# Down projection's operand blocks issued by ScalarE from the second product on, and the out projection's second-half additions with priority

## The chip, the cores and the metric

The kernel runs on one core of one Trainium2 chip. The metric is device microseconds of one execution. Matrix products run on TensorE (PE in the profile), the other arithmetic on VectorE (DVE), ScalarE (ACT) and GpSimd (POOL). Transfers between memory and on-chip buffers are issued here by SyncE (SP, its queue is q1 in the profile) and by ScalarE (queue q10). Each engine runs its own instructions in order, and an instruction waits at its place until what it depends on is done. The time before the change is the median of three runs, 1108.88 us (1105.74 to 1109.55).

## The reference

One layer over 1024 tokens of width 1024: a combined projection feeds two kinds of attention, whose outputs are normed and concatenated (`mix`). After that comes what this study is about:

```python
h = h + jnp.einsum('bse,ed->bsd', mix, w_out[l])
hn = rmsnorm(h, norm_ffn[l])
h = h + conv_gated_mlp(hn, w_gate[l], w_up[l], conv_w[l], conv_b[l], w_down[l])
...
return rmsnorm(h, norm_final)
```

with (the depthwise convolution shortened to one name)

```python
g = jnp.einsum('bsd,df->bsf', h, w_gate)
u = jnp.einsum('bsd,df->bsf', h, w_up)
g = conv_of_width_3(g) + conv_b
return jnp.einsum('bsf,fd->bsd', jax.nn.silu(g) * u, w_down)
```

where `D_FF` is 2816. Everything is float32.

## The kernel before

**Layout and arithmetic.** Activations are held transposed: a tile is 128 features by 1024 tokens, and `tsl(h)` is one half of the tokens (512). A float32 product is made of three fast ones: both operands are split into a high part (ScalarE, a copy that rounds) and a low part (VectorE, the difference), and TensorE does high times high, high times low and low times high (lines 826 to 828 in `group`, 134 to 136 in `block`). So each operand block costs one ScalarE and one VectorE instruction before TensorE may use it.

**Stages.** Attention fills the first 400 us or so. The out projection's second half follows: for each half of the tokens and each of eight output tiles `d`, twelve matmuls go into one PSUM bank (banks with the tags "o", "s" and "pj" in turn, two of each), and `settle_out` adds the bank to the residual `h1` on VectorE (line 845), writes it to memory (ScalarE's queue, line 846) and squares it for the norm (848, 850). Between these, VectorE and ScalarE already scale the first half of the tokens by the norm (855) and split it into operands (833, 834) for the gated MLP, whose first products `p1` write banks "x" with the tag "pj".

The gate and up projections run next over 22 tiles of the wide layer, as seven products instead of eight by sums of halves (a Strassen-Winograd step, with VectorE's additions). Each finished tile is written to memory as operand blocks `X` for the down projection (`keep`, line 1020, on ScalarE's queue).

**The down projection** runs from about 878 us to the end, as seven products again (`PRODUCTS`). Each product is 4 output tiles `j` times 11 operand blocks, in groups `(p, j, c)` of 4, 4 and 3 blocks (`PARTS`), three matmuls per block. The first product goes through all `j` for each part, so that it can begin while its operand blocks are still made; the later ones finish one `j` after another. The second product goes on adding to the banks of the first, after ScalarE has copied the first product out of them (`leave`, line 1254). Later bank contents are added to the residual on VectorE (line 1221).

For each group the loop calls, in program order: `prepare(i + 6, i + 4)`, which issues weight loads (`raw`, line 1107, three buffers) up to six groups ahead and splits weights (815 on ScalarE, 816 on VectorE, nine buffers) up to four groups ahead; the matmuls; the eviction of the group before; a reload of the residual (1207) or its addition (1210); and for the next product `x_load(p + 1, q)` and `x_split(p + 1, q - 1)`. `x_load` brings one block of 128 x 512 into the second half of a buffer `xd` (line 1131), and `x_split` makes the high part (1137, ScalarE) and the low part (1138, VectorE). The `xd` blocks use 22 buffers in turn, so a block for product `p + 1` goes into the buffer of a block of product `p - 1` and waits for TensorE's last use of that.

**What sets the order.** TensorE's order is that of the program, by hand (`manual_schedule`). On every other engine a scheduler decides the order when the program is built; `high_priority` moves an instruction ahead of others that are ready. Transfers from both queues share eight completion counters in turn, so an issue waits for the transfer that used its counter before it.

Of the kernel before, what the change touches and what calls it, by code (L numbers as in the profile page):

```python
# [16 lines left out]
ALU = mybir.AluOpType  # L17
PSUM = bass.MemoryType.PSUM

D, S, HD = 1024, 1024, 64  # L20
KT = D // 128
NB = S // 128
HALF = 512
# [30 lines left out]
def hybrid_layer(tc, xT, w_in, w_out, w_gate, w_up, w_down, small, sink, rpb, consts, rope, out):  # L54
    nc = tc.nc
    with ExitStack() as ctx:
# [13 lines left out]
        def big(name, tag, dt=F32):  # L70
            return lpool.tile([128, S], dt, name=name, tag=tag, bufs=slots[tag])
# [4 lines left out]
        def bank(name, tag):  # L76
            return psum.tile([128, HALF], F32, name=name, tag=tag)

        f32 = lambda ap: ap.bitcast(F32)
# [499 lines left out]
        t = quarters(big("f", "mix"))  # L579
# [106 lines left out]
        for g in range(2):  # L686
            for b in range(NB):
                q, t = unit_window(g, b)
# [49 lines left out]
        for u in range(len(flat)):  # L738
            q, t, need, kind = flat[u]
# [101 lines left out]
        at = lambda k, h: h1[k][:, tsl(h)]  # L841

        def settle_out():
            d, h, ps = late.pop(0)
            nc.vector.tensor_tensor(at(d, h), ps, at(d, h), op=ALU.add)
            nc.scalar.dma_start(spilled[d][:, tsl(h)], at(d, h))
            s2 = half("s2")
            nc.scalar.activation(s2, at(d, h), AF.Square)
            if total[h] is not None:
                nc.vector.tensor_tensor(s2, s2, total[h], op=ALU.add)  # L850
            total[h] = s2
# [34 lines left out]
        for h in range(2):  # L886
            for d in range(KT):
                if h == 0 and d + 2 < KT:
                    wo.append(load_wo(d + 2, fpool))
                ps = bank("pj", ("o", "s", "pj")[(h * KT + d) % 3])  # L890
                for _ in product(ps, wo[d], mg[4:8], h):
                    pass
                late.append((d, h, ps))
                if h == 1 and d == 1:
                    v = inverse_narrow([total[0]], D, "pt")
                settle_out()
                if h == 0 and d in (3, 4):
                    pure((0, FT // 2)[d - 3])
                if h == 0 and d >= 5 or h == 1 and d == 0:
                    head_weights((d - 5) % KT, "s1")  # L900
                if h == 1 and d == 2:
                    wide = widen(v, "pt")
                    normed(0, wide, K1)
                    B[1, 1] = [operand(at(k, 0), "xg") for k in K1]
                if h == 1 and d == 4:
                    normed(0, wide, K2)
                    B[2, 1] = [operand(at(k, 0), "xg") for k in K2]
# [108 lines left out]
        X, first_of = {}, {}  # L1016
# [73 lines left out]
        PRODUCTS = [("11", "11"), ("12", "21"), ("s1", "t1"), ("s2", "t2"), ("s4", "22"), ("s3", "t3"), ("22", "t4")]  # L1090
# [37 lines left out]
        def x_load(p, k):  # L1128
            t = big("xd", "xg" if counts[0] % (2 * FH) < 16 else "op", F32R)
            counts[0] += 1  # L1130
            nc.sync.dma_start(f32(t[:, HALF:S]), X[PRODUCTS[p][1], k])
            xraw[p, k] = t

        def x_split(p, k):
# [18 lines left out]
        for i, f in enumerate(FO[HEAD:]):  # L1153
# [19 lines left out]
            if last_one:  # L1173
                for k in range(4):
                    x_load(0, k)
# [3 lines left out]
            if last_one:  # L1179
                for k in range(4, 6):  # L1180
                    x_load(0, k)
                u.p7()
# [5 lines left out]
            if not last_one:  # L1188
                u.p7()
            else:  # L1190
                for k in range(4):
                    x_split(0, k)
                prepare(4, 2)
                for k in range(6, FH):
                    x_load(0, k)
# [76 lines left out]
        for i, (p, j, c) in enumerate(order):  # L1272
# [6 lines left out]
            ps = banks[p, j]  # L1279
# [26 lines left out]
        for k, cols in enumerate(quarters):  # L1306
            for j in (2, 3):
                ps = banks[6, j]
# [109 lines left out]
```

## Time and profile before

| | |
|---|---|
| time of the profiled execution | 1108.75 us |
| its span | 1106.7 us |
| TensorE's mean granted clock | 0.995 |
| median of three runs | 1108.88 us |
| TensorE idle, 900 to 950 us | 2.76 us |
| TensorE idle, 450 to 460 us | 1.06 us |
| TensorE idle, 1050 us to the end | 7.4 us |
| ScalarE busy, 900 to 950 us | 23.88 us |
| VectorE busy, 470 to 520 us | 49.53 us of 50 |
| ScalarE's waits for `xd` transfers (L1137) | 59.1 us in 35 waits |
| DMA engines' busy share, 900 to 950 us | 0.90, 289 GB/s |
| DMA engines' busy share, 700 to 750 us | 0.30, 101 GB/s |

The profile is of one execution. Busy time leaves out instructions that only wait or issue transfers. A line of the timeline gives the start, the duration, the engine, the source line, the operation and in brackets how long the engine had been idle before it and what released it. A line of the windows gives a stretch of time and its length, then for PE, PEld, DVE, ACT and POOL the busy time and number of instructions, then TensorE's granted clock, the DMA engines' share and GB/s. A line of the waits gives engine, what waited, what it waited for, the sum, how often and the longest. "To landing" is the time from issue of a transfer to its completion.

### The profile page before, as it was taken

To read this page: it belongs to the slowest core of one execution; us is meant where nothing else is said; L and a number is where in the kernel's file an instruction comes from. 1 tells how busy PE (TensorE), PEld (TensorE's weight loads), DVE (VectorE), ACT (ScalarE), POOL (GpSimd) and SP (SyncE) were. 2 spreads that over 40 slices of the span, in tenths; PEclk is the share of its full clock that TensorE was granted. 3 is DMA by queue.
4 is the path that set the end of the run, shared out by engine and by line. 5 is a ranking of instruction groups with operands and counts; after the bars stand their busy time and mean duration, and the time that the engine had idled before them with its cause. 6 is when DMAs were issued, how large, how long until landed. Compare 5 with 4: busy or idle time off the path is not lost.

```text
span 1106.7 us, 15054 instructions
## 1 busy us (share of the span) xinstructions
PE 1082.4 (98%) x5190; PEld 903.6 (82%) x5190; DVE 857.7 (77%) x1565; ACT 551.6 (50%) x1041; POOL 108.7 (10%) x188
## 2 busy tenths in 40 slices
PE   9989999999999999999999999999999999999997
PEld 7868888888888888787788888888888878888887
DVE  7478888667688687899988877877887868886844
ACT  7257766656666544454444334342434644544531
POOL 2213333222232100000000000000000000000001
PEclk9999999999999999999999999999999999999999
DMA  7213122232225237304433222323322889874734
GB/s 270 71 51 79 49 66 65 70 86 67 77 64 156 68 106 264 106 11 145 167 121 127 105 105 96 113 97 116 104 86 105 272 287 300 267 224 159 270 95 153
DMA packets 68364, 144.94 MB, mean 131 GB/s; under 512 B 8128, under 2 KB 18880, under 8 KB 68288
## 3 DMA queue, kind: packets, MB, share of 16 engines
q1 hardware_dynamic: 57632, 118.16, 34.4%
q10 hardware_dynamic: 10656, 25.82, 6.2%
q8 instruction: 40, 0.66, 0.2%
q14 instruction: 36, 0.29, 0.1%
HBM read 103.58 MB, written 28.57 MB: 119 GB/s over the span
## 4 chain that ended last, share of the span: by engine, by line
PE 84%; DVE 9%; DMA 3%; ACT 2%; issue 2%; ACTq 0%; POOL 0%; SPq 0%; DVEq 0%; POOLq 0%
PE dn L826 6%; PE pj L134 6%; PE dn L828 6%; PE dn L827 6%; PE pj L135 6%; PE pj L136 6%; PE z L828 5%; PE z L826 5%; PE z L827 5%; PE s L309 3%; PE x L826 3%; PE x L827 3%; PE x L828 3%; PE y L828 3%; PE y L827 3%; PE y L826 3%
## 5 line engine op out<-in xcount | busy, mean ns | idle before, releaser
L826 PE MATMUL dn<-xd,whi 128*128 128x512 f32 (+1 forms) x330 | 124.9, 378 | 2.8 <-ACT c L1254 2.8
L828 PE MATMUL dn<-xd,wlo 128*128 128x512 f32 (+1 forms) x330 | 124.2, 376 | 0.0
L827 PE MATMUL dn<-xd,whi 128*128 128x512 f32 (+1 forms) x330 | 124.2, 376 | 0.0
L815 ACT ACTIVATE whi<-ws 128x512 fp32r<-128x512 f32 (+1 forms) x100 | 60.1, 623 | 124.1 <-DVE ws L932 82.5
L134 PE MATMUL pj<-xgh,whi 128*128 128x512 f32 x248 | 104.6, 422 | 3.1 <-DVE t L189 3.1
L828 PE MATMUL z<-hg,wlo 128*128 128x512 f32 x264 | 103.1, 390 | 0.6 <-DVE wlo L816 0.6
L826 PE MATMUL z<-hg,whi 128*128 128x512 f32 x264 | 103.0, 390 | 0.2 <-DVE gs L982 0.2
L827 PE MATMUL z<-hg,whi 128*128 128x512 f32 x264 | 102.7, 389 | 0.0
L335 ACT ACTIVATE p<-p,nm 128x385 f32<-128x385 f32 (+3 forms) x128 | 74.9, 586 | 46.9 <-DVE nm L331 46.2
L136 PE MATMUL pj<-xgh,wlo 128*128 128x512 f32 x248 | 98.3, 396 | 0.0
L135 PE MATMUL pj<-xgl,whi 128*128 128x512 f32 x248 | 98.0, 395 | 0.0
L339 POOL TENSOR_SCALAR p<-p,sm 128x384 f32<-128x384 f32 (+1 forms) x128 | 73.4, 586 | 222.0 <-DVE sm L337 207.4
L816 DVE TENSOR_TENSOR wlo<-raw,whi 128x512 fp32r<-128x512 f32 (+1 forms) x102 | 66.3, 670 | 21.8 <-ACT whi L815 20.9
L345 DVE TENSOR_TENSOR pl<-pt,ph 128x384 fp32r<-128x384 f32 (+2 forms) x108 | 63.0, 588 | 24.8 <-ACT ph L344 23.7
L815 ACT ACTIVATE whi<-raw 128x512 fp32r<-128x512 f32 (+1 forms) x102 | 60.4, 611 | 41.7 <-DMA raw<-in_w_down_dram 19.0
L816 DVE TENSOR_TENSOR wlo<-ws,whi 128x512 fp32r<-128x512 f32 (+1 forms) x100 | 66.7, 681 | 18.4 <-ACT whi L815 18.3
L1137 ACT ACTIVATE xd<-xd 128x512 fp32r<-128x512 f32 x77 | 47.1, 627 | 59.4 <-DMA xd<-x 59.1
L1245 POOL TENSOR_TENSOR h<-h,wide 128x256 f32<-128x256 f32 (+1 forms) x6 | 5.4, 925 | 719.8 <-ACT wide L1241 719.8
L826 PEld LDWEIGHTS dn<-xd,whi 128*128 128x128 f32 x330 | 62.5, 189 | 14.2 <-ACT c L1254 3.2
L827 PEld LDWEIGHTS dn<-xd,whi 128*128 128x128 f32 x330 | 62.6, 190 | 11.2
L828 PEld LDWEIGHTS dn<-xd,wlo 128*128 128x128 f32 x330 | 62.4, 189 | 11.4
L344 ACT ACTIVATE ph<-pt 128x384 fp32r<-128x384 f32 (+2 forms) x108 | 55.0, 513 | 32.7 <-PE pt L444 25.2
(209 smaller groups left out, 2687.8 us busy)
## 6 DMA issues: line engine op xcount, KB each, us to landing
xd<-x SPq DMA_DIRECT2D x77, 256.0 KB, 5.0
raw<-in_w_down_dram SPq DMA_DIRECT2D x72, 256.0 KB, 4.1
raw<-in_w_gate_dram SPq DMA_DIRECT2D x22, 512.0 KB, 3.5
raw<-in_w_up_dram SPq DMA_DIRECT2D x22, 512.0 KB, 3.6
x<-c ACTq DMA_DIRECT2D x22, 512.0 KB, 2.6
raw<-in_w_in_dram SPq DMA_DIRECT2D x32, 256.0 KB, 2.8
raw<-in_w_down_dram SPq DMA_DIRECT2D x36, 192.0 KB, 3.9
x<-t ACTq DMA_DIRECT2D x11, 512.0 KB, 2.6
```

What stands on the lines that cost most here:

```text
L134: nc.tensor.matmul(ps, w[0], x[0][:, tsl(h)], start=first, stop=False)
L135: nc.tensor.matmul(ps, w[0], x[1][:, tsl(h)], start=False, stop=False)
L136: nc.tensor.matmul(ps, w[1], x[0][:, tsl(h)], start=False, stop=last)
L335: nc.scalar.activation(p[:, j, 0:e], p[:, j, 0:e], AF.Exp, bias=nm, scale=-1.0, accum_out=sm[:, j:j + 1])
L339: nc.gpsimd.tensor_scalar(p[:, i, 0:m], p[:, i, 0:m], sm[:, i:i + 1], 1.0, op0=ALU.mult, op1=ALU.mult)
L344: nc.scalar.activation(ph[:, 0:n], ps[:, 0:n], AF.Copy)
L345: nc.vector.tensor_tensor(pl[:, 0:n], ps[:, 0:n], f32(ph[:, 0:n]), op=ALU.subtract)
L815: nc.scalar.activation(hi, src, AF.Copy)
L816: nc.vector.tensor_tensor(lo, src, f32(hi[:, :, :]), op=ALU.subtract)
L826: nc.tensor.matmul(ps, w[0], x[0], start=first and i == 0, stop=False, skip_group_check=True)
L827: nc.tensor.matmul(ps, w[0], x[1], start=False, stop=False, skip_group_check=True)
L828: nc.tensor.matmul(ps, w[1], x[0], start=False, stop=last and i == len(ws) - 1, skip_group_check=True)
```

## The change

Two places. In the out projection's second half, the addition of a finished bank to the residual gets a high priority, as the additions of the first half have. In the down projection, the loads of the operand blocks are issued by SP for the first product and by ScalarE for the six others (66 of 77 loads).

```diff
         def settle_out():
             d, h, ps = late.pop(0)
-            nc.vector.tensor_tensor(at(d, h), ps, at(d, h), op=ALU.add)
+            with tc.high_priority(offset=500):
+                nc.vector.tensor_tensor(at(d, h), ps, at(d, h), op=ALU.add)
             nc.scalar.dma_start(spilled[d][:, tsl(h)], at(d, h))
...
         def x_load(p, k):
             t = big("xd", "xg" if counts[0] % (2 * FH) < 16 else "op", F32R)
             counts[0] += 1
-            nc.sync.dma_start(f32(t[:, HALF:S]), X[PRODUCTS[p][1], k])
+            (nc.scalar if p else nc.sync).dma_start(f32(t[:, HALF:S]), X[PRODUCTS[p][1], k])
             xraw[p, k] = t
```

TensorE's and GpSimd's orders are the same in both programs. VectorE's and ScalarE's orders differ in the second half of the out projection and in the down projection, SP's in the down projection.

## The prediction

> **What bounds the kernel now.** I read the page's busy table first, then TensorE's waits, the timeline and the windows round its two largest waits outside the attention, and last the transfers.
>
> ```profile
> PE 1082.4 (98%) x5190; PEld 903.6 (82%) x5190; DVE 857.7 (77%) x1565; ACT 551.6 (50%) x1041; POOL 108.7 (10%) x188
> PE dn L826 <- ACT c L1254: 2.8, 1, 2.8
> PE x L826 <- DVE h L845: 1.1, 1, 1.1
> ```
>
> TensorE is the bound: 98% of 1106.7 us, so idle time is only 24.3 us in all. The two waits are the only ones above 1 us from 400 us on, and each edit touches one: L1254 evicts the down projection's first product, L845 is the addition in the out projection's second half.
>
> ```profile
> 906.82 0.63 ACT L1137 ACTIVATE xd<-xd 128x512 fp32r<-128x512 f32 x1 [2.42 <-DMA xd<-x]
> 909.76 0.63 ACT L1137 ACTIVATE xd<-xd 128x512 fp32r<-128x512 f32 x1 [1.79 <-DMA xd<-x]
> 910.30 0.58 ACT L1254 ACTIVATE c<-dn 128x512 f32<-128x512 f32 x1
> 910.93 0.79 PE L826 MATMUL dn<-xd,whi 128*128 128x512 f32 x1 [2.76 <-ACT c L1254]
> 911.52 0.63 PE L827 MATMUL dn<-xd,whi 128*128 128x512 f32 x1
> 904.00:908.00 4.00, 4.00 (x19) 3.12 (x17) 1.72 (x3) 1.55 (x3) 0.00 (x0) 1.00 0.88 273
> 908.00:912.00 4.00, 1.24 (x4) 0.88 (x4) 2.35 (x5) 2.24 (x5) 0.00 (x0) 0.82 0.86 263
> 912.00:916.00 4.00, 4.00 (x15) 3.22 (x14) 3.49 (x7) 2.92 (x6) 0.00 (x0) 0.75 0.92 284
> ```
>
> The eviction had nothing to wait for but its place: it stands behind operand splits, and these wait for transfers. TensorE starts at 910.93 and not at 908.01 (the last matmul began at 907.78, pitch 0.227). The granted clock then falls to 0.75; the pitch is 0.43 until 913.65. The eighth matmul of the second product starts at 914.05 and would have at 909.60: **4.45 us lost**.
>
> ```profile
> 452.55 2.49 DVE L834 TENSOR_TENSOR hg<-h,hg 128x512 fp32r<-128x512 f32 x4
> 454.96 1.88 DVE L845 TENSOR_TENSOR h<-pj,h 128x512 f32<-128x512 f32 x3
> 456.30 0.50 PE L826 MATMUL x<-hg,whi 128*128 128x512 f32 x1 [1.05 <-DVE h L845]
> ```
>
> Three additions stand behind four operand splits. The second of them frees the bank of the next x product, which starts at 456.30 and not at 455.08: **1.22 us lost**.
>
> **Part one, priority.** No work is added; only VectorE's and ScalarE's order changes. In the built order each of the last six additions stands between the scalings (L855, 0.66 us) and splits (L834, 0.60 us). From the wait at 440.06 I add 0.60 to 0.66 per instruction: the addition of d=6 ends near 452.6, 2.5 us ahead of the need at 455.08. What is pushed back: the last split of the second operand set ends at 457.0 instead of 455.0, and TensorE reaches it at 457.8 plus three blocks of 0.68, 459.8; so that costs nothing, and 2.8 us late it would begin to. The sum of squares for the second norm ends near 460.6; TensorE is there at 460.5 (462.23 before): 0.1 lost. The sums for the next weights now wait for two loads issued behind it, which puts the second norm's reciprocal at 463.6 against a need at 464.2. Bounds: gain 0 (VectorE, 9.9 of 10 us busy from 470 on, returns the wait later) to 1.3. I take **-1.2**, since VectorE's own idle time before 467 (2.65 us at 437, four pieces from 458 to 466) is what shrinks.
>
> **Part two, the queue.** 66 of the 77 operand loads (256 KB) go from SP to ScalarE.
>
> Issue cost: a load of this kind takes 0.32 to 0.43 us on SP; 66 of them are 21 to 28 us of ScalarE over 190 us, where it is half idle (24.3 busy of 50 us at 1000 to 1050). A store issued at 870.76 between splits that start at 870.75 and 871.29 shows no gap at all. 0 to 0.4 each, I take 0.1, hidden by that idle time; without cover 0.4 times 11, 4.4 us per product.
>
> The order costs more. In the built order ScalarE issues block N+1, splits block N (waiting for its landing), splits one set of weights, issues N+2. So two blocks take one landing time L plus one operand split and one weight split (0.55 each in a row of splits):
>
> two blocks = L + 1.1; eleven blocks = 5.5 x (L + 1.1).
>
> A product is 132 matmuls at 0.227, 29.9 us. ScalarE keeps up while L is under **4.3 us**. The same L decides the first transition: from the first such issue (880.2, by the rows of before up to there) to the eviction stand five landings in series, four of operand blocks waited for in their splits and one that a store (L1020) waits for since it reuses the transfer counter, plus 5.9 us of splits and the SiLU: start at 886.1 + 5L, against a need at 907.4. That is again L = 4.3. L = 3.8 gives 905.1 and no wait; 5.0 gives 911.1, 0.8 later than before.
>
> Behind a waiting split stand all later weight splits, the eviction and further loads; TensorE waits for these. Weights are prepared four groups ahead, some 10 us (four times 2.5), which is the cover. On SP the 72 and 36 weight loads come free of the operand loads, but three raw buffers hold them to VectorE's splits: no gain. The sixteen reloads of the residual move earlier, into the first product (4 MB, where 263 to 317 GB/s already run from 896 on); that lengthens L there.
>
> What is L?
>
> ```profile
> DMA to landing us min/median/max: 3.2/5.0/7.6
> 877.30 4.72 SPq L1131 DMA_DIRECT2D xd<-x  x6
> raw<-in_w_down_dram SPq DMA_DIRECT2D x72, 256.0 KB, 4.1
> raw<-in_w_down_dram SPq DMA_DIRECT2D x6, 256.0 KB, 2.9
> ```
>
> The first line is operand loads on SP, issued in bursts (second line) behind one another; the third is weight loads of the same size, the fourth the same at 962 to 975, with no operand loads beside them. Operand loads between 985 and 1010 have a median of 3.8, single ones elsewhere 3.8 to 5.6, mostly behind a run of weight loads. Spread out on another queue, one or two in flight, they lie between 2.9 and 5.0. I take **4.0**, near the 3.8 and 4.1. Then the eviction starts at 906.1, in time: -4.45. The cover in products three to five is thin (5.5 x 5.1 = 28.1 of 29.9 us, and some issues also wait for a weight transfer's counter), so I give back 1.2 for short waits there.
>
> The Trainium skill (DMA: Bandwidth & Descriptors, "Issuing engines are not separate DMA queues") speaks against the edit: loads from either engine share the same sixteen DMA engines, and a second issuer saves issue time alone; by it L stays 5.0, the second rival's time. Its section "Queues, rings and completion order" says the DMA engines take turns between queue rows, by which a load on a nearly empty row would overtake SP's backlog, L nearer 3.5 and 1103.1. No row here has loads on both queues at once, so the trace decides neither.
>
> **Sum.** 1108.75 (the profiled execution: span 1106.7 and 2.05 around it; the median of the runs is 1108.88) - 1.2 - 4.45 + 1.2 = **1104.3**. Nothing removed exceeds 5.67, so 1103.1 is the floor of the mechanism.
>
> **Rivals.**
> 1. *The eviction stays late.* L of 4.5 to 5 in the first product, where share and bytes are highest, then less: start at 908.6 to 911.1, 1.2 to 3.7 late, with the slow clock behind it. For: operand loads issued at 880 to 900 landed after 6.4, at 900 to 925 after 4.9. Against: those were bursts. The gain there is 0 to 2; 1108.75 - 1.2 - 0.5 = 1107.
> 2. *ScalarE paces TensorE* (slower). Place: products three to six, one landing per two blocks; it decides from L = 4.3 sustained. At 5.0 a product takes 33.6 us, 3.7 over; four products 14.8, less the 10 us of cover, 4.8 lost; the eviction 0.8 later too: 1108.75 - 1.2 + 4.8 + 0.8 = 1113.2. For: the median of 5.0, and single loads of 4.8 and 4.9 near 1035 and 1045. Against: products three and four ask for 23 loads per 29.9 us, 5.6 MB or 190 GB/s, below the 270 before 930.
> 3. *Only the second edit works:* VectorE hands the 1.2 back between 510 and 560, where TensorE already waits for it: 1105.5. That the edits do nothing is excluded; the built order shows both.
>
> **How the numbers follow.** Forecast 0.45 (own range 1102.5 to 1106), rival 1 0.17, rival 2 0.33, rival 3 0.05. This kernel's runs spread by 3.8 us, and 0.3% (3.3 us) is about what a measurement can tell from no change: under 1105.4 is faster, over 1112.1 slower at that bound. Faster: 0.42 of the forecast and 0.03 of rival 3, 0.45. Slower: rival 2 where it exceeds 3.3 us, 0.33. Same: 0.22. Range 1102.5 to 1114: from the floor with some scatter up to just above rival 2's value, leaving out its tail (L of 5.5 in all four products is 36.3 us each, 15.6 lost).
>
> **What would show it.** Right: no wait for L1254 near 908, clock 1.00 there, no wait for L845 near 455; operand loads landing in 4.3 or less on ScalarE's queue. Rival 1: the L1254 wait survives. Rival 2: TensorE waits for L815, L816 or L1138 from 970 on, and ScalarE's waits for xd transfers exceed the 59 us of before. The forecast is wrong if TensorE's idle time from 900 to 1050 (2.76 us before) does not shrink.

## The result, and the profile after

The changed kernel takes 1113.34 us in the median of eleven runs (1110.46 to 1116.03), against 1108.76 us for the kernel before on the same chip; the ratio is 1.0048 with an interval of 1.0033 to 1.0063. It is slower by about half a percent, and the interval excludes no change. The profiled execution, 1110.46 us with a span of 1108.7, is the shortest of the eleven, so its profile shows only part of the loss; a second profile of the same kernel (e10 below, 1112.91 us with a span of 1111.1) shows more of it. In the changed kernel every line from 846 on has a number higher by one; the experiments are written so that the numbers of the kernel before hold.

The busy table and TensorE's waits of the changed kernel (columns: engine, what waited, for whom, sum, times, longest):

```profile
PE 1082.6 (98%) x5190; PEld 903.2 (81%) x5190; DVE 857.7 (77%) x1565; ACT 553.2 (50%) x1041; POOL 108.9 (10%) x188
```

```profile
PE dn L826 <- ACT c L1255: 3.1, 1, 3.1
...
PE dn L826 <- ACT xd L1138: 0.7, 1, 0.7
```

TensorE does the same work. The wait for the addition at 455 is gone; the wait for the eviction has grown from 2.8 to 3.1 us, and a new one for an operand block stands behind it. The first edit, in VectorE's timeline of the changed kernel:

```profile
451.58 0.69 DVE L846 TENSOR_TENSOR h<-pj,h 128x512 f32<-128x512 f32 x1
452.19 1.41 DVE L856 SCALAR_TENSOR_TENSOR h<-h,par,sw 128x512 f32<-128x512 f32 x2
453.50 0.70 DVE L834 TENSOR_TENSOR hg<-h,hg 128x512 fp32r<-128x512 f32 x1
454.10 0.70 DVE L846 TENSOR_TENSOR h<-pj,h 128x512 f32<-128x512 f32 x1
```

The additions now come singly between scalings and splits, the one that matters is done at 452.3, and TensorE works without a gap from 450 to 500 (50.00 of 50 us, 48.95 before). The second edit, in ScalarE's timeline of the changed kernel (ACTq is ScalarE issuing a load):

```profile
894.52 0.33 ACTq L1132 DMA_DIRECT2D xd<-x  x1
894.90 0.63 ACT L1138 ACTIVATE xd<-xd 128x512 fp32r<-128x512 f32 x1 [4.19 <-DMA raw<-in_w_down_dram]
...
896.46 0.33 ACTq L1132 DMA_DIRECT2D xd<-x  x1
899.31 0.64 ACT L1138 ACTIVATE xd<-xd 128x512 fp32r<-128x512 f32 x1 [3.37 <-DMA xd<-x]
899.41 0.33 ACTq L1132 DMA_DIRECT2D xd<-x  x1
...
901.97 0.63 ACT L1138 ACTIVATE xd<-xd 128x512 fp32r<-128x512 f32 x1 [1.50 <-DMA xd<-x]
902.43 0.33 ACTq L1132 DMA_DIRECT2D xd<-x  x1
...
903.61 0.64 ACT L1138 ACTIVATE xd<-xd 128x512 fp32r<-128x512 f32 x1
...
904.36 0.35 ACTq L1132 DMA_DIRECT2D xd<-x  x1
908.49 0.63 ACT L1138 ACTIVATE xd<-xd 128x512 fp32r<-128x512 f32 x1 [3.52 <-DMA xd<-x]
...
909.99 0.63 ACT L1138 ACTIVATE xd<-xd 128x512 fp32r<-128x512 f32 x1 [0.31 <-DMA xd<-x]
...
910.53 0.58 ACT L1255 ACTIVATE c<-dn 128x512 f32<-128x512 f32 x1
```

The same stretch of it in windows of 4 us:

```profile
908.00:912.00 4.00, 0.90 (x5) 0.71 (x5) 2.64 (x5) 2.31 (x4) 0.00 (x0) 1.00 1.01 368
912.00:916.00 4.00, 4.00 (x12) 3.15 (x11) 1.78 (x3) 1.17 (x3) 0.00 (x0) 0.57 0.87 257
```

The eviction starts at 910.53, though TensorE stands idle for it from 908.06 on: it stands behind splits that wait for loads issued a few lines further up on the same engine. The load issued at 896.46 is the one split at 901.97, 5.5 us later. In the same way the trace pairs 894.52 with 899.31, 899.41 with 903.61, 902.43 with 908.49 and 904.36 with 909.99: 4.2 to 6.1 us, 5.2 in the mean of the five. TensorE then runs at a granted clock of 0.57 in the mean of the next window. The landing times of the operand loads say how this differs from the rest of the kernel. All 66 loads on ScalarE's queue (the view knows the landing of 27 of them):

```profile
DMA to landing us min/median/max: 2.4/4.1/6.3
```

Those issued from 884 to 912 (known for 3 of 8), and then those from 938 to 968 (4 of 12):

```profile
DMA to landing us min/median/max: 4.8/5.9/6.3
```

```profile
DMA to landing us min/median/max: 3.2/3.4/4.2
```

Over the whole projection a landing takes 4.1 us in the median. The 5.9 rests on three loads, and two of them, issued at 908.50 and 910.00, came too late to hold the eviction up; the five that did are the pairs above. The DMA engines are nearly full there: a share of 0.95 from 884 to 912, and 1.01 in the first window above.

### The profile page after: what moved, and what is told of

Same layout as the page of the kernel before. It is cut to its first block, busy times and chain, and to the rows that moved or that the text cites. A ratio compares the mean times of both kernels' runs of the same rounds, so it can differ in the third digit from the quotient of the medians.

```text
span 1108.7 us, 15034 instructions
## 1 busy us (share of the span) xinstructions
PE 1082.6 (98%) x5190; PEld 903.2 (81%) x5190; DVE 857.7 (77%) x1565; ACT 553.2 (50%) x1041; POOL 108.9 (10%) x188
## 4 chain that ended last, share of the span: by engine, by line
PE 83%; DVE 7%; DMA 5%; ACT 2%; issue 2%; POOL 0%; ACTq 0%; DVEq 0%; SPq 0%; POOLq 0%
PE pj L134 7%; PE pj L135 7%; PE pj L136 7%; PE dn L827 5%; PE dn L828 5%; PE dn L826 5%; PE z L828 5%; PE z L826 4%; PE z L827 4%; PE s L309 3%; PE x L826 3%; PE x L828 3%; PE x L827 3%; PE y L828 3%; PE y L827 3%; PE y L826 3%
## 5 line engine op out<-in xcount | busy, mean ns | idle before, releaser
L816 DVE TENSOR_TENSOR wlo<-ws,whi 128x512 fp32r<-128x512 f32 (+1 forms) x100 | 66.7, 683 | 19.3 <-ACT whi L815 19.3
L816 DVE TENSOR_TENSOR wlo<-raw,whi 128x512 fp32r<-128x512 f32 (+1 forms) x102 | 66.4, 672 | 18.2 <-ACT whi L815 17.3
L1138 ACT ACTIVATE xd<-xd 128x512 fp32r<-128x512 f32 x77 | 47.6, 628 | 59.7 <-DMA xd<-x 51.4
L1139 DVE TENSOR_TENSOR xd<-xd 128x512 fp32r<-128x512 f32 x77 | 52.0, 689 | 30.7 <-ACT xd L1138 26.2
L826 PEld LDWEIGHTS dn<-xd,whi 128*128 128x128 f32 x330 | 62.5, 190 | 15.9 <-ACT c L1255 3.5
```

Of the source, the lines that this page charges most:

```text
L816: nc.vector.tensor_tensor(lo, src, f32(hi[:, :, :]), op=ALU.subtract)
L826: nc.tensor.matmul(ps, w[0], x[0], start=first and i == 0, stop=False, skip_group_check=True)
L1139: nc.vector.tensor_tensor(lo, f32(lo), f32(hi), op=ALU.subtract)
```

## The experiments

"Hand-over" means the step from the first to the second product at 908 us, "tail" the stretch from 1060 us on. The norm's sums (line 171, eight one-column matmuls) are TensorE's first matmuls there that need a square from ScalarE (1225) and its sum (1227). Theory T, formed on the first four runs: ScalarE waits in its own order for the loads that it issued itself; what stands behind a waiting split is late, at the hand-over at once (the eviction), later as a lag that reaches the tail.

One table for all. "Down" is the time from TensorE's first matmul of the down projection to its matmul for the sums, in the profiled execution; "ahead" is how long ScalarE's last operand split starts before TensorE arrives at the sums. Both are subtractions of two timeline starts (less the wait, for "ahead").

| kernel | median us | ratio to before | wait for L1254 | down | wait for L1227 | ahead |
|---|---|---|---|---|---|---|
| before | 1108.76 | 1 | 2.76 | 191.47 | 0 | 19.3 |
| changed | 1113.34 | 1.0048 (1.0033 to 1.0063) | 3.10 | 193.55 | 0 | 17.3 |
| e10, changed again | 1111.83 | 1.0040 (1.0024 to 1.0055) | 4.83 | 196.18 | 1.16 | 15.8 |
| e1 | 1106.68 | 0.9982 (0.9969 to 0.9995) | 2.59 | 189.91 | 0 | 18.9 |
| e2 | 1115.82 | 1.0066 (1.0048 to 1.0085) | 3.19 | 194.71 | 1.92 | 15.9 |
| e3 | 1111.95 | 1.0034 (1.0019 to 1.0049) | 3.56 | 192.49 | 0 | 16.9 |
| e4 | 1109.99 | 1.0022 (1.0006 to 1.0039) | 2.48 | 191.20 | 0 | 19.5 |
| e5 | 1112.82 | 1.0042 (1.0026 to 1.0058) | none | 196.20 | 0 | - |
| e6 | 1120.46 | 1.0112 (1.0093 to 1.0131) | 6.67 | 204.63 | 0 | - |
| e7 | 1109.11 | 1.0014 (1.0003 to 1.0024) | 3.50 | 193.30 | 0 | 22.9 |
| e8 | 1111.80 | 1.0032 (1.0016 to 1.0048) | 4.51 | 194.37 | 0 | 19.3 |
| e9 | 1104.60 | 0.9973 (0.9959 to 0.9987) | none | 188.58 | 0 | 17.5 |
| e11 | 1108.86 | 1.0009 (0.9996 to 1.0022) | 2.11 | 192.57 | 1.28 | 15.8 |
| e12 | 1104.87 | 0.9974 (0.9962 to 0.9987) | none | 191.36 | 0 | 22.7 |

Each ratio is with runs of the kernel before on the same chip (medians of 1107.2 to 1108.8); it is not the quotient of the two medians and differs from that by up to 0.0008, just under a microsecond. The runs of one kernel spread by up to 8 us, so a profile shows where time is lost and the median how much.

### e1 to e4: each edit alone, and which loads cost

e1 is the kernel before with the priority alone; e2 has the loads on ScalarE alone; e3 and e4 have both edits with another condition:

```diff
-            (nc.scalar if p else nc.sync).dma_start(...)
+            (nc.scalar if p > 1 else nc.sync).dma_start(...)      e3
+            (nc.scalar if p == 1 else nc.sync).dma_start(...)     e4
```

> The kernel before with the priority of the additions alone; all loads stay with SP. The two edits together cost 4.6 us in the medians (1108.8 to 1113.3), though the profiled execution of the two showed only 1.7. Theory A (the whole loss lies where the first product of the down projection hands over to the second, 905 to 925 us, in ScalarE's order) and theory B (it is spread over the later products, where ScalarE paces TensorE) both expect the priority to gain its 1.06 us of idle time at 455: about 1107.7, no TensorE wait for the additions, 4.45 us still lost at 908. Theory C (the priority itself costs, by VectorE's order in the gate and up projections, where a new wait of 1.1 us for L983 stands at 868.6) expects 1108.8 or more, and that wait in this profile too.

> The kernel before with ScalarE's issue of the loads from the second product on, without the priority. A and B: the loss of both edits plus the 1.1 that the priority gains, +5.7, about 1114.5, and the new wait for L983 near 868 is here too. C: less than the 4.6 of both, 1112 or under, without that wait.

> Both edits, but the loads of the second product stay with SP as those of the first do, so ScalarE issues 55 loads, from the third product on. A: the hand-over is as in the kernel before or better (eviction L1254 at 910.3 or sooner), the later products cost nothing: 1107.7 or less. B: four products still paced by ScalarE, 1111 or more, with TensorE waits for L815, L816 or L1138 from 950 on. In between (the loads of the third product are the ones that reach into 905 to 925): 1109 to 1110.

> Both edits, but ScalarE issues the loads of the second product alone (11 loads); from the third on SP does. A: the late eviction and the second wait at 919 to 923 stay, 1112 to 1113.5. B: 1108 or less. If the second wait (operand blocks issued behind the evictions) comes from the third product's loads in between, only the first stays: about 1108 to 1109.

The priority alone gains (1106.68 against 1107.84 us for the kernel before beside it), so theory C falls; the queue alone costs 8.0 us (1115.82 against 1107.84), where both together cost 4.6. Neither A nor B holds as stated: the second product's loads alone cost 3.3 us over e1, those from the third on 5.3, and together with the priority they cost 6.7 (1113.34 less 1106.68), less than the two added. In e3, whose second product's loads are SP's, the eviction is late all the same (TensorE waits 3.56 us, 2.59 in e1). The profile of e4 is of one of its shorter runs and shows 0.5 us more idle time at the hand-over than that of e1, so the place of its 3.3 us is argued from which loads moved, not shown. The profile of e2, whose execution was the longest of that kernel (1116.25 us), names a place that neither theory had. TensorE's timeline of e2 at the sums, and then its windows there:

```profile
1073.69 1.86 PE L171 MATMUL ss<-ones,s 128*128 128x1 f32 x8 [1.92 <-DVE s L1227]
```

```profile
1070.00:1074.00 4.00, 2.08 (x10) 1.44 (x8) 2.82 (x5) 2.19 (x4) 0.00 (x0) 0.97 0.49 138
1074.00:1078.00 4.00, 4.00 (x14) 3.52 (x14) 2.17 (x5) 3.12 (x5) 0.00 (x0) 0.50 0.18 50
```

The sum of squares comes 1.92 us too late, and the clock is 0.50 in the next window and until 1080.55, for 6.8 us in all. Between 940 and 1060 us TensorE has no gap in e2 or e3 (20.00 of 20 us in every window): the lag is there, but hidden until the tail.

The new wait for L983 (L982 in the experiments) at 868 us stands in the changed kernel (1.1), e2, e3 and, with the loads on SP, in e5 (1.1), and shorter in e4 (0.6) and e11 (0.3), but not in e1, e6, e7, e8, e9 or e12. In e10, the same program as the changed kernel, it is 0.2 as in the kernel before, and the first moved load is issued at 869.84, after it, so it is not the change; why it comes and goes stays open.

### e5 and e6: no operand split on ScalarE at all

```diff
-            nc.scalar.activation(hi, f32(lo), AF.Copy)
+            (nc.gpsimd.tensor_copy(hi, f32(lo)) if p else nc.scalar.activation(hi, f32(lo), AF.Copy))
```

in `x_split`, with the priority; loads on SP in e5, on ScalarE in e6.

> The priority edit, loads with SP, and the high part of the operand blocks (from the second product on) made by GpSimd in place of ScalarE, so that nothing on ScalarE waits for an operand block. Theory T (ScalarE's splits wait for landings, and whatever stands behind them in its order is late): the eviction L1254 no longer stands behind such a split, TensorE's wait of 2.6 us near 908 shrinks below 1 us and the clock stays 1.00 there: 4.45 us less than the priority alone (1106.7), about 1102.5. Rival (the eviction is late for another reason, such as weight loads, or GpSimd is too slow for 11 blocks in 30 us): 1106 or more, and TensorE waits for xd L1137 or L1138.

> Both edits, and the same move of the high parts to GpSimd: ScalarE issues 66 loads but waits for none of them in a split. T: the last square of the sixth and seventh product is no longer late, the wait for L1227 of e2 (1.9 us and half clock behind it) can't come back, and the second wait near 920 goes: 1107 or less. Rival I (issuing from ScalarE costs in itself: 66 issues, and waits for transfer counters ahead of weight splits and evictions): 1111 or more, about what both edits cost now (1113.3).

In e5 the wait for the eviction is gone, as T says, but the time is 10 us over the expected: the cure costs elsewhere. TensorE's waits, VectorE's timeline and GpSimd's timeline of e5:

```profile
PE dn L828 <- DVE wlo L816: 5.1, 6, 1.7
```

```profile
985.70 1.67 DVE L1138 TENSOR_TENSOR xd<-xd 128x512 fp32r<-128x512 f32 x2 [0.51 <-POOL xd L1137]
988.01 1.07 DVE L1138 TENSOR_TENSOR xd<-xd 128x512 fp32r<-128x512 f32 x1 [0.65 <-POOL xd L1137]
989.01 1.09 DVE L816 TENSOR_TENSOR wlo<-sum,whi 128x512 fp32r<-128x512 f32 x1
```

```profile
987.37 7.70 POOL L1137 CAST xd<-xd 128x512 fp32r<-128x512 f32 x9 [1.14 <-DMA xd<-x]
```

GpSimd makes nine blocks in a row, VectorE now waits for these with the weights' low parts behind, and most of its 128x512 subtractions take 1.07 to 1.09 us instead of 0.69 meanwhile. e6 was a clear miss of T: with no operand split on ScalarE the eviction is later still, and TensorE waits 6.67 us for it. ScalarE's timeline of e6:

```profile
908.22 0.63 ACT L815 ACTIVATE whi<-raw 128x512 fp32r<-128x512 f32 x1 [0.94 <-ACT whi L815]
911.66 0.33 ACTq L1131 DMA_DIRECT2D xd<-x  x1
912.16 0.52 ACT L815 ACTIVATE whi<-raw 128x384 fp32r<-128x384 f32 x1 [3.31 <-DMA h<-h1d]
912.59 0.58 ACT L1254 ACTIVATE c<-dn 128x512 f32<-128x512 f32 x1
```

Here it is the issue that waits: the load at 911.66 needs the completion counter that a reload of the residual (`h<-h1d`) on SP's queue still holds, and the eviction stands behind it. So T had to be widened: ScalarE waits for transfers not only in the splits, but in the issues too. Rival I was half right: the cost of issuing is not the 0.33 us of the instruction, but the wait for a counter.

### e7 and e8: the lag

e7 is the changed kernel with each split called two places behind its load instead of one; e8 gives the loads of the last two products back to SP (`0 < p < 5`).

```diff
-                if q >= 1:
-                    x_split(p + 1, q - 1)
+            if i >= 2 and (i - 2) % 12 < FH and (i - 2) // 12 + 1 < len(PRODUCTS):
+                x_split((i - 2) // 12 + 1, (i - 2) % 12)
```

> Both edits, with the split of a block called two places behind its load in place of one, so that two loads are in flight on ScalarE's queue. T: ScalarE's waits for operand blocks (51.4 us after) fall below 35, its last split of the down projection comes before 1045 (1054.2 after, 1042.9 with SP's loads), and the time is 1107 to 1110. Rival I: 1112 or more with the waits gone. Rival D (a landing takes longer the more loads are in flight, so the waits stay): the waits stay above 45 us and the time above 1111.

> Both edits, but SP issues the loads of the last two products. T: ScalarE makes up its lag before the last products, the squares there are in time and TensorE doesn't wait for L1227 near 1071; what is left is the loss at the hand-over alone, as with the second product alone on ScalarE (1110): 1109 to 1111. If the tail's loss does not come from ScalarE's lag in the last products: 1113 or more, like both edits in full.

ScalarE's waits of e7:

```profile
ACT xd L1137 <- DMA xd<-x: 32.9, 31, 4.2
```

With each split one place later the waits fall from 51.4 to 32.9 us, the last split is 22.9 us ahead of the sums instead of 15.8 to 17.3, and 4.2 us of the median come back (2.7 against the 1111.83 of e10, the same changed kernel); what e7 still loses to e1 (2.4 us) its profile shows at the hand-over alone, with a wait of 3.50. That is T's lag, met in all its numbers but one: the last split starts at 1048.0, not before 1045. In e8 the tail is free as expected (19.3 ahead, no wait), but the hand-over waits 4.51 us, and the median is 0.8 above what T allowed.

### e9 and e11: the two places apart

In the order that the scheduler builds, the splits right ahead of the first eviction belong to the third product, which TensorE reaches 30 us later; their loads were ready sooner than the last two of the second product. (e1 has 24 operand splits on ScalarE ahead of the eviction, e9, which moves the third product's, 20.) e9 is e1 with GpSimd making the high parts of those eleven blocks alone (`if p == 2`). e11 has both edits with ScalarE's loads from the fourth product on (`p > 2`), which leaves the hand-over as in e1.

> The priority edit, loads with SP, and GpSimd makes the high parts of the third product's operand blocks alone (11 blocks). These are the blocks whose splits stand ahead of the eviction L1254 on ScalarE although TensorE needs them 30 us later. Theory T: the wait of 2.6 us near 908 and the slow clock behind it go, as in e5, and the later products (where e5 lost 5.1 us behind weights that VectorE made late) are as with the priority alone: 1106.7 - 4 = 1102.5. Rival: another thing is late at the same place (weights of the second product, behind raw loads): 1105 or more.

> Both edits as they are, for another profile, since the first was of the shortest of its eleven runs. T: the time near the median (1113), with the wait for L1254 at 908, and either a longer wait there (e8 had 4.5 us), a second wait near 920 (0.9 us in the first profile) or one at the norm's sums near 1071 (1.9 us in e2); no TensorE waits between 925 and 1060. Rival 2 as predicted (ScalarE paces TensorE in products three to six): waits for L815, L816 or L1138 between 950 and 1060.

> Both edits, but ScalarE issues the loads from the fourth product on (44 loads); SP's order up to 938 is that of the priority alone. T has two parts, the hand-over at 908 and ScalarE's lag of up to 12 us in the later products, which shows at the tail alone. So the hand-over is that of the priority alone, ScalarE's last split is again 4 us or more later against TensorE's end, and the time is 1107 to 1109.5. If the lag costs nothing by itself: 1106.7. If it costs all of the 5.3 that the loads from the third product on cost in e3: 1111 to 1112.

ScalarE's timeline of e9:

```profile
904.63 0.53 ACT L815 ACTIVATE whi<-raw 128x384 fp32r<-128x384 f32 x1 [1.43 <-DMA raw<-in_w_down_dram]
905.06 0.58 ACT L1254 ACTIVATE c<-dn 128x512 f32<-128x512 f32 x1
```

The eviction runs at 905.06, in time; only 0.7 us of short waits for operand blocks are left up to 916, the clock stays 1.00, and the median is 1104.60, 2.1 us under e1. T said 4, with a slow clock behind the wait that e1's profile does not show. It beats both kernels of this study, its interval excludes no change, and it moves no load.

e10's timeline of TensorE at the sums, and then the stretch of slow clock behind them:

```profile
1072.20 1.05 PE L171 MATMUL ss<-ones,s 128*128 128x1 f32 x8 [1.16 <-DVE s L1227]
```

```profile
1074.25:1077.65 3.40, 3.40 (x10) 2.62 (x9) 1.87 (x4) 2.38 (x4) 0.00 (x0) 0.50 0.01 2
```

Both places lose in one execution of the changed kernel: at the hand-over TensorE waits 4.83 us, 2.76 before. At the tail the loss is 1.16 of waiting and 1.70 of slow clock (18 matmuls from 1073.12 to 1078.91 take 5.79 us; at a pitch of 0.227 it would be 4.09). With 0.42 us of gaps between 1040 and 1060, and less the 1.06 gained at 455, that makes 4.3 of the 4.4 us by which the span of e10 exceeds that of the kernel before. e11 has the tail's part alone: no worse hand-over than e1 (2.11), a last split only 15.8 us ahead, a wait of 1.28 for the sums, and 2.2 us over e1, within T's range. From e11 to e3 only the third product's eleven loads go to ScalarE as well. That costs 3.1 us in the medians, and it lies at the hand-over: the wait grows from 2.11 to 3.56 us, and the clock behind it falls (0.81 and 0.77 in the windows from 908 and 912, 1.00 in e11).

### e12: both places cured

e11's loads, e9's third product on GpSimd and e7's later splits in one kernel.

> Both edits with ScalarE issuing the loads from the fourth product on (as e11), the third product's high parts on GpSimd (as e9), and every split called two places behind its load (as e7). T (the whole loss of the loads on ScalarE is waiting for landings in its order, at the hand-over and at the tail): no wait for L1254 near 908, none for L1227 near 1071, ScalarE's last split before 1050, and the time is that of e9, 1104.6, within a microsecond. Rival I (44 issues on ScalarE cost something in themselves): 1106 or more, without those two waits.

1104.87 us, 0.3 from e9: with the waits for L1254 and L1227 gone, 44 loads on ScalarE cost nothing that can be measured, and they gain nothing either. (Its profiled execution, the longest of the twelve and 191.36 us in the table, has 2.04 us of waits for operand blocks between 912 and 916.) Two things are left open. The later splits were not run without the moved loads, so a gain of their own could hide a cost of the loads. And no run leaves all 66 loads on ScalarE and has the eviction in time, so how the changed kernel's loss at the hand-over divides between waiting splits and waiting issues is not shown.

## Why the prediction was wrong

**Part one, priority: right.** The idle time of 1.06 us at 455 is gone, VectorE does not hand it back (49.16 of 50 us busy on TensorE from 500 to 550, 49.19 before), and the median of e1 is 1.2 us under the kernel before (0.3 to 3.4 by the interval of the ratio). Rival 3's condition did not occur.

**Part two, issue cost: right in itself, wrong in kind.** The instruction costs 0.33 us, and e12 finds no cost of 44 of them. (The instruction at 871.29 that the prediction took for a split is line 971's; that changes nothing.) What the prediction priced once, for the store, and otherwise only named, is the wait of an issue for its completion counter. In the changed kernel 4.19 us of idle ScalarE stand ahead of the load issued at 894.52: by the trace its counter is held by a weight load on SP's queue, issued at 887.62, which lands at 894.50. In e6 such a wait, there for a reload of the residual, is the last thing ahead of the eviction.

**The step that failed: "886.1 + 5L ... L taken 4.0 ... Then the eviction starts at 906.1, in time: -4.45".** The term L was mis-sized. Measured, the eviction started at 910.53 and in e10 at 910.31. The five operand loads whose splits stand last ahead of it took 5.2 us in the mean until their splits began (5.3 in e10), not 4.0; with 5.2 the prediction's own sum gives 912.1, late, where 4.0 gave 906.1, in time. L is 4.1 over the loads of all products, as taken, but the decision falls between 894 and 910. The prediction had the reason in front of it, more reloads of the residual in the first product, and rows for it (6.4 at 880 to 900, which rests on one load, and 4.9 at 900 to 925, on four), and set them aside because those loads came in bursts. One number for a whole stage was the mistake: the term had to be sized at the place where it decides.

That the sum with the measured L comes within 2 us is partly luck, since its form did not hold as stated. The five landings are not in series; two loads are often in flight at once. From 880.2 to the eviction, 30.3 us, ScalarE idles 8.8 us for operand blocks, 4.2 for the counter of the issue at 894.52 and 4.7 for VectorE. Most of the rest is its own work, where the sum had 5.9 us for work and nothing for VectorE. The 4.45 us did not come back but grew: from the first matmul of the projection to the sums TensorE needs 193.55 and 196.18 us, 191.47 before. That the blocks in the way belonged to the third product (e9, and e3 over e11) was not seen either.

**The cover, "give back 1.2": it held where the prediction looked, and the lag showed elsewhere.** Between 940 and 1060 TensorE's gaps stay at 0 and 0.42 us in the two profiles (the 0.42 is two waits for L816, rival 2's sign at a tenth of its price), so rival 2's place is wrong. Its mechanism is not: the 22nd, 33rd, 44th and 55th of ScalarE's 77 operand splits, eleven to a product, fall behind the kernel before by 5, 7, 10 and 12 us (908.49, 934.29, 968.08, 997.87 against 903.24, 927.44, 957.75, 985.79), which is the four groups of cover and more. The cover is not refilled in time: at the end squares and sums stand among weight splits, which wait for their own loads (five times 0.4 to 1.6 us from 1058 to 1068 in e10). In the three profiles in which the last operand split is 15.8 or 15.9 us ahead of the sums (e2, e10, e11), TensorE waits 1.2 to 1.9 us there and loses 1.7 to 3.4 us more to the clock; at 16.9 us and more it does not wait. Rival 2's time (1113.2) came out by chance: by rival 1's late eviction, which cost more than the 1107 of that rival, and this tail, not by rival 2's own sum. Its sign, ScalarE's waits for operand blocks above 59 us, would have misled: they fell to 51.4 while the lag grew, since waiting at a place with nothing late behind it costs nothing.

The sum, corrected by the runs: 1108.8 - 1.2 (e1) + 2.2 (tail, e11 over e1) + 3.3 (hand-over, e4 over e1) = 1113.1, against 1113.34 and 1111.83 measured. It is a sum of medians of different kernels, good to about a microsecond, and it counts the hand-over once: the third product's loads cost 3.1 there (e3 over e11) and the second product's 3.3 by themselves (e4), but both make the same eviction late, and they do not add.

The Trainium skill's rule that the prediction set aside (DMA: Bandwidth & Descriptors, "Issuing engines are not separate DMA queues": loads share the same DMA engines whoever issues them) is borne out where it mattered: the five loads on ScalarE's queue took 4.2 to 6.1 us with the DMA engines nearly full, no less than SP's loads issued from 880 to 925 in the kernel before (4.1 to 6.4 for the five whose landing is known). From 938 to 968, with a share of 0.82 (0.95 from 884 to 912), landings on ScalarE's queue took 3.4. The share does not explain all: the last loads of e10, issued after 1028 at a share of 0.67, took 6.2 in the median of the three known, and why is open.

## What to carry to other kernels

An engine that computes should not issue loads that it waits for a few instructions later, or its use of them should be moved back (e7, e12): each landing, and each wait for a completion counter held by someone else's transfer, then stands ahead of everything that the engine owes to others. Size a landing time in the stretch where it decides, not by the median of a stage. If an eviction is late behind operand splits, look up in the built order whose operands they are: here moving the splits that were not needed for another 30 us gained more than moving any load.

## What the runs showed of the hardware

**A short idle time is enough for the slow clock, but not always, and the slow stretch comes in pieces of 3.4 us.** At the hand-over TensorE idled 2.59 us (e1), 2.48 (e4) and 2.11 (e11) with a granted clock of 1.00 behind it; after 2.76 (before) and 3.10 (changed) it fell to 0.50. At the tail 1.16 (e10), 1.28 (e11) and 1.92 us (e2) sufficed, with about one microsecond of one-column matmuls right behind the wait. The clock then stayed at 0.50 for 3.4 us, in e2 for twice that, and 1.7 us (in e2 3.4) were lost. The 0.75 before and the 0.57 of the changed kernel are the same 3.4 us, spread differently over windows of 4 us. What decides between a gap that costs the clock and one that does not, these runs do not show. The Trainium skill (TensorE: Matmul & The Clock Gate, "What's actually happening") gives an idle window of about 3.4 us; here less was enough.

**GpSimd's casts slow VectorE.** While GpSimd made nine 128x512 blocks in a row (e5), VectorE's subtractions of that size took mostly 1.07 to 1.09 us instead of 0.69.
